# Twice the descriptor space for GpSimd's transfers, with a sum moved into a gate tile and a gate kept in PSUM

## The chip, the cores and the metric

The kernel runs on one core of a Trainium2 chip. The core has a matrix engine (TensorE), a vector engine (VectorE), a scalar engine (ScalarE), a general-purpose engine (GpSimd) and a synchronising engine (SyncE). They run side by side and wait for one another through semaphores. Data come from HBM by DMA; the transfers are started by SyncE, ScalarE or GpSimd and moved by 16 DMA engines. On the chip, data lie in SBUF (128 partitions) or in the 8 banks of PSUM, where TensorE puts its results. The metric is the device time of one execution in microseconds; less is better. The profile calls the engines PE (with PEld for its weight loads), DVE, ACT, POOL and SP.

## The reference

A trunk of two layers over 256 frames of 2048 channels. Layer 0 mixes the frames by gated linear attention, layer 1 by sparse attention over selected frames; behind each mixer stands a feed-forward block, and at the end a norm:

```python
for i in range(DEPTH):                      # DEPTH = 2
    h = rmsnorm(x, norm_mix[i])
    y = gla_mixer(h, ...) if i % 2 == 0 else dsa_mixer(h, ...)
    x = x + y
    x = x + swiglu(rmsnorm(x, norm_ffn[i]), ffn_w1[i], ffn_w3[i], ffn_w2[i])
return rmsnorm(x, norm_final)

def swiglu(h, w1, w3, w2):
    return (jax.nn.silu(h @ w1) * (h @ w3)) @ w2
```

w1 and w3 are 2048 x 5632, w2 is 5632 x 2048, all in float32. The change touches only the feed-forward block, `swiglu`.

## The kernel before

The program runs in order through gated attention (`gla`), feed-forward (`ffn`), sparse attention (`dsa`), feed-forward again, and the final norm; in the profile the two feed-forward stages lie at about 300 to 1080 us and 1460 to 2235 us. The program is written for a framework that places tiles, sets all semaphores and decides the order in which each engine gets its instructions. A pool gives out tiles by tag; tiles of one tag share its buffers, and a new one waits until the last reader of an older one is done.

Every product of float32 matrices is made of three matmuls on rounded halves. `split_w` (lines 133 to 141) makes the halves of a weight block of 512 x 512: ScalarE casts it to `wh` (line 137), VectorE subtracts to get `wl` (line 138). Both have three buffers; `raw` blocks that come from HBM have four (`RAW`).

The 5632 columns of w1 and w3 are cut into eleven blocks of 512. Two of them (1 and 5) are computed plainly by `plain_steps`. The other nine go through `pair` (lines 372 to 455), which computes h @ w1 and h @ w3 for both 128-row halves of the frames with seven products instead of eight, by sums and differences of the operands, in the manner of Strassen and Winograd. The forms of h that this needs (A11, A12, N7, F5, F6, F3, N22) are made once in `NormF.group`, where the tile f5 (line 327) is one of the helpers. The sums of weight blocks are made on the fly, half by half (c = 0, 1):

- `va` and `vb` are loaded (lines 423, 424); `plus` adds vb to va on VectorE (line 410).
- Product F5 uses va. As each half has been split, `plus_dma` (lines 417, 418) lets GpSimd start a DMA that adds another block of w3 to that half in place. Its result feeds product F6.
- `vc` and `vd` are streamed through `raw` (lines 435, 438). `minus` turns vb into another sum on VectorE (line 414).
- Product F6 uses va again, and again each half gets a block of w1 added by `plus_dma`, for product N22.

So each of the nine turns starts four accumulating transfers of 1 MB from GpSimd, two behind F5 and two behind F6. Over the two layers that is 36 pairs, 72 transfers.

The seven products collect in three PSUM banks, `b1`, `b2` and `b3`, out of four. The tile `y` (lines 432, 433) takes a copy of b2 after F5, and b3 is added to it after N7 (line 449). `gate` (lines 556 to 564) then makes silu(h @ w1) * (h @ w3): `done("11", b1)` and `done("12", w)` for the first 128 rows, `done("21", b3)` and `done("22", y)` for the second. It writes into tiles of tag "u" (two buffers, 2048 bytes a partition each). The gated tiles are transposed on TensorE (line 219, `split_t`) during the next turn and later multiplied with w2 in `pieces` (lines 515 to 538; matmuls 530 to 532). Between the products of a pair, `ffn` runs pieces or plain steps at slots listed in `turns`, so that TensorE has other work while sums are made.

Before the change, y has a buffer of its own of tag "y" in the pool of the stage (2048 bytes a partition), which f5 uses earlier. The program is built with `dynamic_dma_scratch_size=2048` (line 1158): the bytes a partition that are set aside for the descriptors of GpSimd's transfers.

Of the kernel before, what the change touches and what calls it, by code (L numbers as in the profile page):

```python
# [12 lines left out]
F32 = mybir.dt.float32  # L13
F32R = mybir.dt.float32r
BF16 = mybir.dt.bfloat16
AF = mybir.ActivationFunctionType
ALU = mybir.AluOpType
AX = mybir.AxisListType

P = 128  # L20
# [3 lines left out]
NB = 512  # L24
# [31 lines left out]
def trunk(  # L56
# [7 lines left out]
    nc = tc.nc  # L64
# [4 lines left out]
    cm = ctx.enter_context(tc.tile_pool(name="cm", bufs=2))  # L69
# [47 lines left out]
    def tick():  # L117

        while side:
            try:  # L120
                return next(side[0])
            except StopIteration:
                side.popleft()
# [9 lines left out]
    def split_w(raw, pool=wp):  # L133

        wh = pool.tile([P, 4, NB], F32R, tag="wh", bufs=3 if pool is wp else 1, name="wh")
        wl = pool.tile([P, 4, NB], F32R, tag="wl", bufs=3 if pool is wp else 1, name="wl")
        nc.scalar.copy(wh, raw)  # L137
        nc.vector.tensor_sub(wl, raw, wh.bitcast(F32))  # L138
        if sums_due:
            sums_due.popleft()()  # L140
        return wh, wl
# [83 lines left out]
    class Norm:  # L225
# [20 lines left out]
        def group(self, n):  # L246
            hi, lo = self.homes[n]
            for kk in range(2):
                tr = tr_p.tile([P, 2, SEQ], F32, tag="tr", name="tr")
                for t in range(NT):  # L250
                    for k in range(2):
                        c = (2 * kk + k) * P
                        nc.tensor.transpose(tr[:, k, t * P:(t + 1) * P], x[t][n][:, c:c + P], ident)
                gs = [cols[:, c:c + 1] for c in range(self.g0 + 4 * n + 2 * kk, self.g0 + 4 * n + 2 * kk + 2)]
                for k, g in enumerate(gs):
                    kt = 2 * kk + k
                    a = nc.scalar.activation(hi[:, kt, :], tr[:, k, :], AF.Copy, scale=g)
                for k, g in enumerate(gs):
                    kt = 2 * kk + k
                    v = nc.vector.scalar_tensor_tensor(lo[:, kt, :], tr[:, k, :], g, hi[:, kt, :].bitcast(F32),  # L260
                                                       op0=ALU.mult, op1=ALU.subtract)
                self.last = (a.ins, v.ins)
                if kk == 1:
                    self.parts[n] = (hi, lo, n * NB)
                yield
# [10 lines left out]
    class NormF(Norm):  # L276
# [21 lines left out]
        def group(self, n):  # L298
            j, c = divmod(n, 2)
            if c == 0:  # L300
                self.hx[j] = self.pool.tile([P, 2, 4, SEQ], F32, tag=("v0", "v1")[j], bufs=1, name="hx")
            for kk in range(2):
                tr = tr_p.tile([P, 2, SEQ], F32, tag="tr", name="tr")
                for t in range(NT):
                    for k in range(2):
                        f = (2 * kk + k) * P
                        nc.tensor.transpose(tr[:, k, t * P:(t + 1) * P], x[t][n][:, f:f + P], ident)
                for k in range(2):
                    col = self.g0 + 4 * n + 2 * kk + k
                    nc.scalar.activation(self.hx[j][:, c, 2 * kk + k, :], tr[:, k, :], AF.Copy,  # L310
                                         scale=cols[:, col:col + 1])
                yield
            a11, a21 = (self.hx[0][:, c, :, t * P:(t + 1) * P] for t in range(NT))

            def form(tag, l_, r_):
                f = self.pool.tile([P, 4, P], F32, tag=tag, bufs=1, name="form")
                nc.vector.tensor_sub(f, l_, r_)
                return f

            if j == 0:  # L320
                self.split("A11", c, a11)
                yield
                self.split("N7", c, form("s1", a11, a21))
                yield
                return
            a12, a22 = (self.hx[1][:, c, :, t * P:(t + 1) * P] for t in range(NT))
            f5 = form("y", a21, a22)
            self.split("F5", c, f5)
            f6 = form("w", a11, f5)
            self.split("A12", c, a12)  # L330
            yield
            self.split("F6", c, f6)
            f3 = form("s1", a12, f6)
            self.split("F3", c, f3)
            self.split("N22", c, a22, True)
            yield
# [35 lines left out]
    def pair(nrm, wa, wb, c0, turn, done):  # L372

        def src(w, j, c):
            r = j * 1024 + c * 512
            return w[r:r + 512, c0:c0 + NB].rearrange("(k p) n -> p k n", p=P)

        def load(w, j, homes):  # L380
            o = []
            for c, (pool, tag, bufs) in enumerate(homes):
                raw = pool.tile([P, 4, NB], F32, tag=tag, bufs=bufs, name=tag)
                nc.sync.dma_start(raw, src(w, j, c))
                o.append(raw)
            return o

        def product(acc, raws, form, start, stop, then=None):
            for c in range(2):
                wh, wl = split_w(raws[c])  # L390
                if then is not None:
                    then(c)
                hi, lo = nrm.forms[form]
                for j in range(4):
                    k = 4 * c + j
                    for i, (l_, r_) in enumerate(((hi, wh), (hi, wl), (lo, wh))):
                        nc.tensor.matmul(acc, l_[:, k, :], r_[:, j, :], start=start and k == i == 0,  # L397
                                         stop=stop and k == 7 and i == 2, skip_group_check=not start)
                    if j % 2:
                        tick()  # L400

        def bank():
            return acc_p.tile([P, NB], F32, tag="acc", name="acc")

        def sums(tag):
            return nrm.pool.tile([P, NB], F32, tag=tag, bufs=1, name=tag)

        def plus(dst, other):

            return lambda c: sums_due.append(lambda: nc.vector.tensor_add(dst[c], dst[c], other[c]))  # L410

        def minus(dst, other):

            return lambda c: sums_due.append(lambda: nc.vector.scalar_tensor_tensor(
                dst[c], dst[c], -1.0, other[c], op0=ALU.mult, op1=ALU.subtract))

        def plus_dma(dst, w, j):
            return lambda c: nc.gpsimd.dma_start(dst[c], src(w, j, c), accum_op=ALU.add)  # L418

        fz = nrm.pool  # L420
        stream = [(wp, "raw", RAW)] * 2
        homes = [((fz, "v0", 1), (fz, "v1", 1)), ((fz, "v2", 1), (res, "g3", 1))]
        va = load(wa, 0, homes[turn])
        vb = load(wb, 0, homes[1 - turn])
        b1 = bank()
        product(b1, va, "A11", True, True, plus(va, vb))
        b3 = bank()
        nc.scalar.mul(b3, b1, -1.0)
        yield
        b2 = bank()  # L430
        product(b2, va, "F5", True, True, plus_dma(va, wb, 1))
        y = sums("y")
        nc.scalar.copy(y, b2)
        yield
        vc = load(wb, 1, stream)
        product(b2, vc, "F3", False, True, minus(vb, vc))
        yield
        vd = load(wa, 1, stream)
        product(b1, vd, "A12", False, True)
        done("11", b1)  # L440
        yield
        product(b3, va, "F6", False, True, plus_dma(va, wa, 1))
        w = sums("w")
        nc.scalar.copy(w, b3)
        nc.vector.tensor_add(w, w, b2)
        done("12", w)
        yield
        product(b3, vb, "N7", False, True)
        nc.vector.tensor_add(y, y, b3)
        yield  # L450
        product(b3, va, "N22", False, True)
        done("21", b3)
        done("22", y)
        yield
        yield
# [84 lines left out]
    def ffn(layer, nrm):  # L540

        w1, w3, w2 = ffn_w1[layer], ffn_w3[layer], ffn_w2[layer]
        sc = {}
# [12 lines left out]
        def gate(us):  # L556
            def done(q, v):
                t = int(q[0]) - 1
                if q[1] == "1":
                    us[t] = cm.tile([P, NB], F32, tag="u", name="u")  # L560
                    nc.scalar.activation(us[t], v, AF.Silu, scale=sc["n" if t else "r"][:, t:t + 1])
                else:
                    nc.vector.scalar_tensor_tensor(us[t], us[t], sc["r"][:, t:t + 1], v, op0=ALU.mult, op1=ALU.mult)
            return done
# [28 lines left out]
        for turn, (b, at, items) in enumerate(turns):  # L593
            todo.extend(filler(i) for i in items)
            us = [None] * NT
# [573 lines left out]
```

## Time and profile before

| | us |
|---|---|
| median of 3 runs (2270.14 to 2272.52) | 2271.91 |
| the profiled execution | 2270.45 |
| its span, first to last instruction | 2268.6 |
| feed-forward of layer 0 (300 to 1080) | 780 |
| feed-forward of layer 1 (1460 to 2235) | 775 |

The profile gives for each engine the busy time. Idle time of an engine is put down to what ended it ("<-"). "DVE wl L138" is VectorE's instruction of line 138 that writes wl. A DMA's issue stands on the engine that issued it; the data land later. TensorE's matmuls overlap one another by a part of their length, so that a 512-column matmul is listed with about 0.39 us and follows the one before by 0.23. A row of a timeline has the start, the duration, engine, line, operation, what is written and read, the number of instructions merged into it, and in brackets the idle time before it and what ended it.

### The profile page before, as it was taken

The page shows a single profiled execution, that of the slowest core. Times are in us where ns is not written, and L with a number is a line of the kernel's source. Part 1 is how long each engine was busy: PE and PEld are TensorE (multiplying, and loading weights), DVE is VectorE, ACT ScalarE, POOL GpSimd, SP SyncE. Part 2 cuts the span into 40 slices and gives each one's busy share as a digit, 9 for nine tenths or more (in the row PEclk, how much of TensorE's full clock was granted, in tenths as well). Part 3 has the DMA queues.
Part 4 walks back from the last instruction along what each step waited for, and adds up shares of the span by engine and source line. Part 5 has one row for each costly group of instructions (what it writes and reads, how often), then busy time and mean ns, then how long its engine had stood idle before and what let it go on. Part 6 is the DMA issues. An engine that isn't in the chain of part 4 may idle for free. (4 is left out here: it accounts for less than half of the span.)

```text
span 2268.6 us, 25156 instructions
## 1 busy us (share of the span) xinstructions
PE 2218.0 (98%) x10151; PEld 1821.4 (80%) x10151; DVE 1585.1 (70%) x1200; ACT 1338.1 (59%) x1326; POOL 122.1 (5%) x165
## 2 busy tenths in 40 slices
PE   9999999999999999999999999999999999999997
PEld 7888888877888887777888888888787888787876
DVE  6546456887788778777655755558778787887785
ACT  5545355756666766666544544456576666666664
POOL 0000000100000000000100000000000000000000
PEclk9999999999999999999999999999999999999998
DMA  8555465887988798778554555557898889787973
GB/s 288 169 171 190 127 231 185 264 227 234 312 234 238 241 296 246 229 249 223 191 167 150 184 168 167 168 190 214 240 301 229 248 252 299 216 242 240 300 220 109
DMA packets 258998, 501.74 MB, mean 221 GB/s; under 512 B 8329, under 2 KB 20961, under 8 KB 258753
## 3 DMA queue, kind: packets, MB, share of 16 engines
q1 hardware_dynamic: 219856, 423.33, 53.4%
q0 software_dynamic: 38016, 75.50, 19.1%
q8 instruction: 79, 1.29, 0.2%
q10 hardware_dynamic: 1008, 1.31, 0.2%
q14 instruction: 39, 0.31, 0.0%
HBM read 497.98 MB, written 2.12 MB: 220 GB/s over the span
## 5 line engine op out<-in xcount | busy, mean ns | idle before, releaser
L138 DVE TENSOR_TENSOR wl<-raw,wh 128x2048 fp32r<-128x2048 f32 x185 | 421.1, 2289 | 165.3 <-ACT wh L137 164.0
L196 DVE TENSOR_TENSOR wl<-raw,wh 128x2048 fp32r<-128x2048 f32 (+3 forms) x147 | 317.6, 2164 | 276.0 <-ACT wh L195 275.9
L137 ACT CAST wh<-raw 128x2048 fp32r<-128x2048 f32 x185 | 353.4, 1913 | 140.3 <-PE half L474 39.2
L195 ACT CAST wh<-raw 128x2048 fp32r<-128x2048 f32 (+3 forms) x147 | 264.8, 1806 | 218.2 <-PE acc L207 197.7
L138 DVE TENSOR_TENSOR wl<-v,wh 128x2048 fp32r<-128x2048 f32 x132 | 300.6, 2287 | 63.5 <-ACT wh L137 63.1
L205 PE MATMUL acc<-wh,hh 128*128 128x512 f32 (+3 forms) x832 | 325.4, 391 | 0.0
L207 PE MATMUL acc<-wh,hl 128*128 128x512 f32 (+3 forms) x832 | 317.4, 381 | 0.0
L206 PE MATMUL acc<-wl,hh 128*128 128x512 f32 (+3 forms) x832 | 316.4, 380 | 0.6 <-DVE wl L196 0.6
L137 ACT CAST wh<-v 128x2048 fp32r<-128x2048 f32 x132 | 251.9, 1913 | 87.5 <-DVE v L410 24.9
L531 PE MATMUL down<-wl,g 128*128 128x512 f32 x640 | 250.6, 391 | 5.6 <-DVE wl L138 5.5
L530 PE MATMUL down<-wh,g 128*128 128x512 f32 x640 | 248.6, 392 | 2.6 <-ACT down L520 2.6
L532 PE MATMUL down<-wh,g 128*128 128x512 f32 x640 | 249.3, 389 | 0.0
L206 PEld LDWEIGHTS acc<-wl,hh 128*128 128x128 f32 x832 | 156.7, 188 | 29.6 <-issue 1.7
L207 PEld LDWEIGHTS acc<-wh,hl 128*128 128x128 f32 x832 | 156.3, 188 | 29.3
L205 PEld LDWEIGHTS acc<-wh,hh 128*128 128x128 f32 x832 | 156.5, 188 | 28.6 <-issue 1.9
L397 PE MATMUL acc<-wl,fhF 128*128 128x512 f32 x432 | 169.9, 393 | 7.3 <-DVE wl L138 7.3
L397 PE MATMUL acc<-wh,fhF 128*128 128x512 f32 x432 | 171.4, 397 | 4.2 <-ACT wh L137 2.4
L397 PE MATMUL acc<-wh,flF 128*128 128x512 f32 x432 | 168.4, 390 | 0.0
L138 DVE TENSOR_TENSOR wl<-g,wh 128x2048 fp32r<-128x2048 f32 x48 | 109.8, 2287 | 60.9 <-ACT wh L137 60.7
L531 PEld LDWEIGHTS down<-wl,g 128*128 128x128 f32 x640 | 120.1, 188 | 34.2 <-DVE wl L138 10.1
L530 PEld LDWEIGHTS down<-wh,g 128*128 128x128 f32 x640 | 120.1, 188 | 31.8 <-ACT down L520 7.0
L537 ACT COPY x<-down 128x512 f32<-128x512 f32 x112 | 65.4, 584 | 130.9 <-PE down L532 130.6
(283 smaller groups left out, 3776.7 us busy)
## 6 DMA issues: line engine op xcount, KB each, us to landing
raw<-in_ffn_w SPq DMA_DIRECT2D x192, 1024.0 KB, 7.7
v<-in_ffn_w SPq DMA_DIRECT2D x54, 1024.0 KB, 9.7
v<-in_ffn_w POOLq DMA_DIRECT2D x52, 1024.0 KB, 9.7
raw<-in_dsa_w_in SPq DMA_DIRECT2D x48, 1024.0 KB, 4.9
raw<-in_gla_w_in SPq DMA_DIRECT2D x40, 1024.0 KB, 5.1
g<-in_ffn_w POOLq DMA_DIRECT2D x20, 1024.0 KB, 13.2
g<-in_ffn_w SPq DMA_DIRECT2D x18, 1024.0 KB, 6.5
raw<-in_gla_w_out SPq DMA_DIRECT2D x16, 1024.0 KB, 5.0
```

The source lines that it names most:

```text
L137: nc.scalar.copy(wh, raw)
L138: nc.vector.tensor_sub(wl, raw, wh.bitcast(F32))
L195: a = nc.scalar.copy(wh[:, sl, :n], raw[:, sl, :n])
L196: v = nc.vector.tensor_sub(wl[:, sl, :n], raw[:, sl, :n], wh[:, sl, :n].bitcast(F32))
L205: nc.tensor.matmul(acc[t][:, :n], hi[:, k, ts_], wh[:, k, :n], start=start, stop=False)
L206: nc.tensor.matmul(acc[t][:, :n], hi[:, k, ts_], wl[:, k, :n], start=False, stop=False)
L207: nc.tensor.matmul(acc[t][:, :n], lo[:, k, ts_], wh[:, k, :n], start=False, stop=last)
L397: nc.tensor.matmul(acc, l_[:, k, :], r_[:, j, :], start=start and k == i == 0, stop=stop and k == 7 and i == 2, skip_group_check=not start)
L530: nc.tensor.matmul(acc[t], hi[:, k, ts_], wh[:, k, :], start=False, stop=False, skip_group_check=True)
L531: nc.tensor.matmul(acc[t], hi[:, k, ts_], wl[:, k, :], start=False, stop=False, skip_group_check=True)
L532: nc.tensor.matmul(acc[t], lo[:, k, ts_], wh[:, k, :], start=False, stop=last, skip_group_check=True)
L537: nc.scalar.copy(x[t][n], acc[t])
```

## The change

The space for descriptors goes from 2048 to 4096 bytes a partition. The tag "y" of the stage's pool goes: f5 and y take a tile of tag "u" from the pool `cm`, which has two buffers. The gate of the second 128 rows no longer takes a tile of "u": silu is applied in the PSUM bank b3 itself, and the product is written over y, which is then what gets transposed. The instructions are the same in kind and number.

```diff
-            def form(tag, l_, r_):
-                f = self.pool.tile([P, 4, P], F32, tag=tag, bufs=1, name="form")
+            def form(tag, l_, r_, pool=None):
+                f = (pool or self.pool).tile([P, 4, P], F32, tag=tag, bufs=2 if pool else 1, name="form")
                 nc.vector.tensor_sub(f, l_, r_)
                 return f
...
-            f5 = form("y", a21, a22)
+            f5 = form("u", a21, a22, cm)
...
         product(b2, va, "F5", True, True, plus_dma(va, wb, 1))
-        y = sums("y")
+        y = cm.tile([P, NB], F32, tag="u", name="u")
         nc.scalar.copy(y, b2)
...
             def done(q, v):
                 t = int(q[0]) - 1
-                if q[1] == "1":
+                if q == "21":
+                    nc.scalar.activation(v, v, AF.Silu, scale=sc["n"][:, 1:2])
+                    us[t] = v
+                elif q == "22":
+                    nc.vector.scalar_tensor_tensor(v, v, sc["r"][:, 1:2], us[t], op0=ALU.mult, op1=ALU.mult)
+                    us[t] = v
+                elif q[1] == "1":
                     us[t] = cm.tile([P, NB], F32, tag="u", name="u")
                     nc.scalar.activation(us[t], v, AF.Silu, scale=sc["n" if t else "r"][:, t:t + 1])
                 else:
                     nc.vector.scalar_tensor_tensor(us[t], us[t], sc["r"][:, t:t + 1], v, op0=ALU.mult, op1=ALU.mult)
...
-    nc = bacc.Bacc("TRN2", target_bir_lowering=False, num_devices=1, dynamic_dma_scratch_size=2048)
+    nc = bacc.Bacc("TRN2", target_bir_lowering=False, num_devices=1, dynamic_dma_scratch_size=4096)
```

## The prediction

> **What bounds the kernel now.** I read the page first, then the engine windows of the two feed-forward stages, TensorE's waits, and the timeline around single waits.
>
> ```profile
> span 2268.6 us, 25156 instructions
> PE 2218.0 (98%) x10151; PEld 1821.4 (80%) x10151; DVE 1585.1 (70%) x1200; ACT 1338.1 (59%) x1326; POOL 122.1 (5%) x165
> ...
> q0 software_dynamic: 38016, 75.50, 19.1%
> ```
>
> TensorE bounds the whole. Only its 50.6 us of idle time (2268.6 - 2218.0) can be won, since the change takes no matmul away. The change touches the two stages that run `ffn`:
>
> ```profile
> 300.00:1080.00 780.00, 763.48 (x3397) 623.60 (x3396) 593.36 (x341) 498.30 (x437) 48.92 (x42) 1.00 0.82 244
> 1460.00:2235.00 775.00, 756.88 (x3351) 616.53 (x3349) 587.43 (x339) 497.52 (x444) 48.08 (x38) 1.00 0.82 241
> ```
>
> Behind the stretch and its length stand the busy times of TensorE, its weight loads, VectorE, ScalarE and GpSimd, the granted clock, the DMA share and GB/s. TensorE idles 16.5 + 18.1 = 34.6 us there, at a granted clock of 1.00. Its waits name the causes:
>
> ```profile
> PE acc L397 <- DVE wl L138: 10.9, 12, 1.8
> PE acc L397 <- ACT wh L137: 6.3, 8, 2.6
> PE tr L219 <- DVE u L563: 5.5, 2, 2.8
> PE down L531 <- DVE wl L138: 5.5, 6, 1.2
> ...
> PE down L530 <- ACT down L520: 2.6, 3, 1.5
> ```
>
> wh and wl are the two halves of a weight block, made by ScalarE (L137) and VectorE (L138). To see why they are late I follow one wait back, from GpSimd's accumulating transfers (L418) to TensorE.
>
> ```profile
> 2172.07 2.28 DVE L138 TENSOR_TENSOR wl<-g,wh 128x2048 fp32r<-128x2048 f32 x1
> ...
> 2172.56 1.31 POOL L418 DMA_DIRECT2D v<-in_ffn_w  x1 [36.55 <-DVE wl L138]
> 2181.48 1.29 POOL L418 DMA_DIRECT2D g<-in_ffn_w  x1 [7.61 <-DMA v<-in_ffn_w]
> ...
> DMA to landing us min/median/max: 8.6/11.0/13.3
> ...
> 2194.88 1.91 ACT L137 CAST wh<-g 128x2048 fp32r<-128x2048 f32 x1 [2.98 <-DMA g<-in_ffn_w]
> ...
> 2196.82 2.29 DVE L138 TENSOR_TENSOR wl<-g,wh 128x2048 fp32r<-128x2048 f32 x1 [2.48 <-ACT wh L137]
> ...
> 2199.17 0.50 PE L397 MATMUL acc<-wl,fhF 128*128 128x512 f32 x1 [0.71 <-DVE wl L138]
> ```
>
> Each product issues two such transfers of 1 MB, one for each half. The second could go when wl of g is done, at 2172.07 + 2.28 = 2174.35. It goes at 2181.48, 0.3 us after the first landed (2172.56 + 8.6), though it writes another tile. It lands at 2181.48 + 13.3 = 2194.8; ScalarE has stood for it 2.98 us, cast and subtraction follow, and TensorE waits 0.71 us. All 36 pairs look so: no second transfer starts before the first has landed. GpSimd has room for one at a time. That is the resource the change doubles.
>
> **The sum of waits that hang on it.** Of the 23 waits of L397 and L530 (10.9 + 6.3 + 2.6 = 19.8 us) twelve stand directly behind the landing of a second transfer: at 466.0 and 468.3, the last at 2199.17, 16.0 us together. The other eleven, 3.8 us, are each under 0.7 us, and no landing precedes them.
>
> ```profile
> 465.96 0.51 PE L397 MATMUL acc<-wh,fhN 128*128 128x512 f32 x1 [2.64 <-ACT wh L137]
> 468.29 0.68 PE L397 MATMUL acc<-wl,fhN 128*128 128x512 f32 x1 [1.82 <-DVE wl L138]
> ```
>
> **Doubling the space.** By the trace one transfer fits in 2048 bytes, so two fit in 4096. In the example the second is issued some 6.5 us earlier: 2174.35 + about 0.6 (2172.56 was 0.4 behind its own subtraction; the first's 1.3 us of issue lie ahead of it). How much earlier it lands depends on the DMA engines:
>
> ```profile
> 2174.60:2181.20 6.60, 6.38 (x31) 4.99 (x30) 6.60 (x5) 5.22 (x5) 0.00 (x0) 1.00 1.05 172
> 2181.20:2185.70 4.50, 4.50 (x22) 3.72 (x20) 3.16 (x2) 1.58 (x3) 1.29 (x1) 1.00 0.99 331
> 2185.70:2194.80 9.10, 9.10 (x41) 7.37 (x40) 6.70 (x3) 6.13 (x5) 0.00 (x0) 1.00 1.08 274
> ```
>
> The engines are full throughout: first the accumulating transfer almost alone (172), then SyncE's loads alone (331), then both (274). Issued early, the second follows the first at 2181.2 and shares from there. Bounds: 0 earlier, if the loads stay first, to 6.5, the hold itself. If it gets the share of the third stretch, it needs the same 9.1 us and lands 4.5 us earlier, the length of the loads' own stretch; if the loads' backlog takes half of that back, 2.3. I take 3.5, between them. Then the twelve waits end so: the pair at 466/468 (4.46) loses 3.5; all others are at most 3.1 together at one landing and go. Recovered: 16.0 - 1.0 = **15.0 us**.
>
> The Trainium skill says, in "DMA: Bandwidth & Descriptors", section "Issuing engines are not separate DMA queues", that transfers of all issuing engines run on the same 16 DMA engines and that starting them from several engines saves only the time of initiating. By that rule a full DMA would give the loads' time back in full, and the sum would be near 0; the 1.05, 0.99 and 1.08 agree that it is full here.
>
> **What the loads lose.** The price is theirs. In the third stretch 274 x 9.1 = 2.49 MB moved, 1.05 of them the transfer's, 1.44 the loads'. A load of 1 MB beside it therefore takes 9.1 x 1.05 / 1.44 = 6.6 us of that stretch.
>
> ```profile
> 2179.42 0.37 SPq L384 DMA_DIRECT2D raw<-in_ffn_w  x1
> ...
> DMA to landing us min/median/max: 5.0/5.0/5.0
> ...
> 2185.71 3.72 ACT L137 CAST wh<-raw 128x2048 fp32r<-128x2048 f32 x2
> ...
> 2187.65 4.50 DVE L138 TENSOR_TENSOR wl<-raw,wh 128x2048 fp32r<-128x2048 f32 x2 [3.29 <-ACT wh L137]
> ...
> 2192.86 0.39 PE L397 MATMUL acc<-wl,fhA 128*128 128x512 f32 x1
> ```
>
> This load lands at 2184.4 now, and at 2181.2 + 6.6 = 2187.8 then. Its cast, the second of the two, starts at 2185.71 + 3.72 - 1.91 = 2187.5 anyway; its wl ends at 2192.15 and is needed at 2192.86. So it bears 3.1 + 0.7 = 3.8 us, and loses 3.4: no wait, with 0.4 to spare. Ten loads of `vd` lie so, the first at 421.83; at 0 to 0.5 us each, I charge 0.3, **3 us** in all.
>
> **Waits that stay.** The six of L531 (5.5 us) come from a third load:
>
> ```profile
> 814.84 1.91 ACT L137 CAST wh<-raw 128x2048 fp32r<-128x2048 f32 x1 [5.96 <-DMA raw<-in_ffn_w]
> ...
> 804.42 6.82 DVE L138 TENSOR_TENSOR wl<-raw,wh 128x2048 fp32r<-128x2048 f32 x3 [0.73 <-ACT wh L137]
> ...
> 815.15 0.39 PE L397 MATMUL acc<-wl,fhA 128*128 128x512 f32 x1
> ...
> 804.30:814.00 9.70, 9.70 (x44) 8.05 (x43) 6.79 (x3) 4.33 (x4) 0.00 (x0) 1.00 1.06 269
> ```
>
> By 814.84 both accumulations and three loads must be through full engines (1.06), in whatever order. I count 0 for these; 5.5 is the upper end. The two waits of L219 (5.5) are the end of a stage and stay.
>
> **The moved tiles.** No instruction is added or taken away.
>
> ```profile
> L563 DVE SCALAR_TENSOR_TENSOR u<-u,rstd,y 128x512 f32<-128x512 f32 x18 | 13.4, 746 | 1.3 <-ACT u L561 1.3
> ...
> L489 DVE SCALAR_TENSOR_TENSOR early<-early,rstd,half 128x512 f32<-128x512 f32 x4 | 3.0, 741 | 0.0
> ...
> L433 ACT COPY y<-acc 128x512 f32<-128x512 f32 x18 | 10.6, 588 | 14.1 <-PE acc L397 14.1
> L428 ACT ACTIVATE acc<-acc 128x512 f32<-128x512 f32 x18 | 10.5, 581 | 5.9 <-PE acc L397 5.6
> ```
>
> The gate of the second half (L563) will read PSUM: L489 does so in 741 ns against 746. Silu will write PSUM: L428 writes it in 581 ns, L433 SBUF in 588. 0 us. Two lifetimes grow. y takes a buffer of "u" until the transposes (L219) have read it, so the next `copy` (L433) waits for them; behind it on ScalarE stand the casts. The bank of b3 is held until L563, and the next F5 product may need it.
>
> ```profile
> 2175.20 0.60 PE L219 MATMUL tr<-ident,u 128*128 128x128 f32 x4
> ...
> 2178.59 0.59 ACT L433 COPY y<-acc 128x512 f32<-128x512 f32 x1 [0.80 <-PE acc L397]
> ...
> 2084.11 0.75 DVE L563 SCALAR_TENSOR_TENSOR u<-u,rstd,y 128x512 f32<-128x512 f32 x1
> ...
> 2089.13 0.50 PE L397 MATMUL acc<-wh,fhF 128*128 128x512 f32 x1 [0.35 <-ACT wh L137]
> ```
>
> These are the narrowest places: 2.8 us from transposes to copy, 4.3 us from gate to product. Both are covered: 0 us. The f5 tile gets a second buffer and nothing waits for it.
>
> **Sum.** 15.0 - 3 = 12 us off the profiled execution's 2270.45 us (span 2268.6 and 1.85 around it): 2258.5. The median of the runs, 2271.91, is 1.46 above that execution, so 2271.91 - 12 = **2260 us**.
>
> **Rivals.** *Full engines, only the order changes.* The loads give back what the transfers win: the loads' delay passes 3.8 us by about 1.5 at the ten places (15 us), and nothing is left. For it: DMA shares of 0.99 to 1.08. Against: the twelve waits are few and the loads have slack. 2272.
>
> *Slower: the second transfer keeps the loads out.* If it goes wholly ahead, it needs 1.05 MB at 172, 6.1 us behind 2181.2, and the load 2.7 more (1.05 MB at 388 GB/s, where loads run alone): it lands at 2190.0 instead of 2184.4, 5.6 late. That is 1.8 us over the 3.8, at ten places 18. At the six places of L531 the second load has no more than the 3.9 us between its wl, the third of the row at 804.42 (ended 811.24), and the matmul at 815.15: 1.7 over, 10 more. 28 - 15 = 13 us slower: 2285. It decides from a delay of 3.8 us. Against: loads and transfer shared the third stretch, 1.44 MB to 1.05.
>
> ```profile
> 800.40:804.30 3.90, 3.90 (x19) 3.21 (x18) 3.29 (x2) 3.42 (x5) 1.30 (x1) 1.00 1.03 388
> ```
>
> *The space is not what holds it.* Then nothing changes: 2272. For it: the hold might be a semaphore. Against: the second transfer writes another tile than the first. A transfer leaves 38016 / 72 = 528 packets, 33 on each DMA engine. The Trainium skill ("DMA: Bandwidth & Descriptors", "The descriptor swizzle") has 9 read and 9 write descriptors per engine for 1 MiB, of 16 bytes ("Terms"); an estimate from it puts seven such transfers in 2048 bytes, and by that this rival would hold. The 33 packets contradict its count here.
>
> *All goes.* The twelve waits and L531's: 16.0 + 5.5 = 21.5 less: 2250.
>
> **Chances.** Forecast (2254 to 2267) 0.65, all goes 0.08, full engines 0.11, space not the hold 0.05, slower 0.11. 0.2% is 4.5 us, about what a measurement of this kernel can tell from no change. Faster 0.73, same 0.16, slower 0.11. The range goes from 2250 to 2272: it takes in the cases of no change, and leaves out the slower one.
>
> **What would show it.** Right: second transfers issued 2 to 4 us behind the first, before it lands; in the accumulating pairs ScalarE's casts of v and g no longer wait for DMA; L397 <- wh, wl and L530 <- L520 fall from 19.8 to some 5 us; L531 stays near 5.5. Loads of `vd` landing over 3.8 us later speak for the slower rival. Unchanged gaps of 8 to 9 us between the two issues mean that the space was not the hold. A copy of y that waits for L219, or an F5 product that waits for L563, would show the moved tiles wrong. The order of each engine's instructions is fixed when the program is built; if the new buffers change it, other waits of a few us may come or go, and the sum is off by them.

## The result, and the profile after

The changed kernel takes 2260.06 us (median of 4 runs, 2258.83 to 2260.71) against 2272.22 for the kernel before beside it: a ratio of 0.9946, 95% interval 0.9929 to 0.9963, or 8 to 16 us. The two profiled executions differ by 9.7 us (2270.45 and 2260.71, spans 2268.6 and 2258.9). Each engine gets the same instructions in the same order in both programs, but for a transpose in each feed-forward stage, three small loads of the attention stage and a block of the last product, which stand a few places earlier or later; the gate of the second 128 rows writes and reads other tiles, as the change has it. So the difference is one of waiting.

The profile page of the kernel after: its span, busy times and the queue of GpSimd's transfers:

```profile
span 2258.9 us, 25154 instructions
...
PE 2216.3 (98%) x10151; PEld 1821.7 (81%) x10151; DVE 1585.6 (70%) x1200; ACT 1340.9 (59%) x1326; POOL 121.7 (5%) x165
...
q0 software_dynamic: 38016, 75.50, 19.2%
```

TensorE idles 42.6 us instead of 50.6. The same two stretches in the engine windows (TensorE's busy time is the second number):

```profile
300.00:1080.00 780.00, 766.13 (x3411) 626.02 (x3410) 596.15 (x343) 500.21 (x438) 48.69 (x42) 1.00 0.82 246
1460.00:2235.00 775.00, 761.95 (x3365) 621.44 (x3365) 589.97 (x342) 496.76 (x438) 47.87 (x38) 0.99 0.81 242
```

More matmuls fit into each stretch (3411 and 3365, before 3397 and 3351). TensorE's waits after (total, times, longest):

```profile
PE acc L397 <- DVE wl L138: 14.6, 20, 1.5
PE tr L219 <- DVE u L563: 5.8, 3, 2.7
...
PE acc L397 <- ACT wh L137: 2.3, 6, 0.6
PE acc L397 <- ACT u L433: 1.8, 8, 0.2
PE down L531 <- DVE wl L138: 1.4, 2, 0.7
```

L530's waits are gone, L531's fell from 5.5 to 1.4, L397's for wh from 6.3 to 2.3. But L397's for wl **rose**, from 10.9 to 14.6. The four groups were 25.3 us and are 18.3. The groups of L397 by form show that these are not the same waits. Behind the bar stand the idle time ahead of the group and what ended it; fhF is read by F3, F5 and F6, fhA by A11 and A12, fhN by N7 and N22. The kernel before:

```profile
L397 PE MATMUL acc<-wl,fhF 128*128 128x512 f32 x432 | 169.9, 393 | 7.3 <-DVE wl L138 7.3
...
L397 PE MATMUL acc<-wl,fhA 128*128 128x512 f32 x288 | 113.7, 395 | 0.0
L397 PE MATMUL acc<-wl,fhN 128*128 128x512 f32 x288 | 113.7, 395 | 3.6 <-DVE wl L138 3.6
...
L397 PE MATMUL acc<-wh,fhN 128*128 128x512 f32 x288 | 113.4, 394 | 3.9 <-ACT wh L137 3.9
```

The kernel after:

```profile
L397 PE MATMUL acc<-wl,fhF 128*128 128x512 f32 x432 | 168.9, 391 | 1.3 <-DVE wl L138 1.3
...
L397 PE MATMUL acc<-wl,fhA 128*128 128x512 f32 x288 | 116.3, 404 | 13.3 <-DVE wl L138 13.3
...
L397 PE MATMUL acc<-wh,fhN 128*128 128x512 f32 x288 | 112.0, 389 | 0.0
L397 PE MATMUL acc<-wl,fhN 128*128 128x512 f32 x288 | 112.0, 389 | 0.0
```

F6 and N22, which use what the transfers bring, no longer wait; what is left at fhF are small waits that both kernels have. A12, which uses the loads of `vd`, and A11 never waited and now wait 13.3 us: A12 10.6 at thirteen places, A11 1.3 at each of two (473.34 and 1621.92). Some of what such waits cost stands as busy time, too: the group of 288 has 116.3 us instead of 113.7.

A wait can also cost something behind itself. In the kernel before, this is the stretch right behind N22's waits of 2.64 and 1.82 us, the second of which ends at 468.29:

```profile
468.50:471.90 3.40, 3.40 (x9) 2.66 (x9) 3.37 (x2) 1.49 (x1) 0.00 (x0) 0.51 0.72 224
```

The granted clock is 0.51 there, and in the timeline the matmuls follow one another by 0.43 us instead of 0.23. By an estimate from this row it costs 3.4 x 0.5 = 1.7 us. In the kernel after, the clock of this stretch is 1.00. In the second layer both kernels have such a stretch: before 0.50 from 1622.2, behind N22's waits; after 0.51 from 1622.7, behind A11's wait of 1.33 us. The mean of 1.00 over a whole stage does not show them.

The turn of the prediction's example, in the timeline of the kernel after:

```profile
2163.88 1.28 POOL L418 DMA_DIRECT2D v<-in_ffn_w  x1 [42.84 <-DVE wl L138]
2166.07 1.28 POOL L418 DMA_DIRECT2D g<-in_ffn_w  x1 [0.92 <-DVE wl L138]
...
2170.74 0.37 SPq L384 DMA_DIRECT2D raw<-in_ffn_w  x1
...
2180.45 1.91 ACT L137 CAST wh<-raw 128x2048 fp32r<-128x2048 f32 x1 [1.47 <-DMA raw<-in_ffn_w]
...
2182.39 2.29 DVE L138 TENSOR_TENSOR wl<-raw,wh 128x2048 fp32r<-128x2048 f32 x1 [1.09 <-ACT wh L137]
...
2184.74 0.50 PE L397 MATMUL acc<-wl,fhA 128*128 128x512 f32 x1 [0.39 <-DVE wl L138]
```

The second transfer goes 2.2 us behind the first (before: 8.9). The trace has its landing at 2179.23, 15.4 us behind the first's issue (before: 22.2). Over the 18 pairs behind F5 the median fell from 22.5 to 16.4 us, behind F6 from 23.0 to 16.3. The load of `vd`, issued 6.9 us behind the first transfer in both kernels, lands 16.5 us behind it (2180.35) instead of 11.9 (2184.4): 4.6 later, 0.8 beyond the 3.8 it could bear, and TensorE waits 0.39.

The DMA queues of the kernel after from 2174.9 to 2178.2, packets, MB and share of time of each queue, show how the two share (q0 carries GpSimd's transfers, q1 SyncE's loads):

```profile
DMA packets 427, 0.87 MB, mean 263 GB/s; under 512 B 3, under 2 KB 3, under 8 KB 427
...
q0 software_dynamic: 210, 0.42, 69.1%
q1 hardware_dynamic: 217, 0.44, 40.1%
```

The two move packet for packet, 210 to 217, but an accumulating packet takes 69.1 / 210 against 40.1 / 217 of the time, 1.8 times as long. Beside a transfer the loads get 0.44 MB in 3.3 us, 133 GB/s, a third of what loads get alone (388). The Trainium skill says in "DMA: Bandwidth & Descriptors", section "Queues, rings and completion order", that each DMA engine takes the queues that have work in turn, a packet from each; the 210 and 217 agree.

### The profile page after: what moved, and what is told of

The parts are those of the page before. It is cut to its first block, busy times and chain, and to the rows that moved or that the text cites. A ratio compares the mean times of both kernels' runs of the same rounds, so it can differ in the third digit from the quotient of the medians.

```text
span 2258.9 us, 25154 instructions
## 1 busy us (share of the span) xinstructions
PE 2216.3 (98%) x10151; PEld 1821.7 (81%) x10151; DVE 1585.6 (70%) x1200; ACT 1340.9 (59%) x1326; POOL 121.7 (5%) x165
## 4 chain that ended last, share of the span: by engine, by line
PE 71%; DVE 12%; DMA 8%; issue 5%; ACT 4%; SPq 0%; POOL 0%; ACTq 0%; DVEq 0%; POOLq 0%
PE acc L397 17%; PE acc L205 11%; PE acc L207 11%; PE acc L206 11%; DMA raw<-in_ffn_w 7%; DVE wl L138 7%; PE half L474 5%; PE down L530 4%; PE down L531 4%; PE down L532 4%; ACT wh L137 3%; DVE v L410 2%; DVE v L414 1%; PE trq L906 0%; PE po L765 0%
## 5 line engine op out<-in xcount | busy, mean ns | idle before, releaser
L531 PE MATMUL down<-wl,g 128*128 128x512 f32 x640 | 249.6, 390 | 1.4 <-DVE wl L138 1.4
L530 PE MATMUL down<-wh,g 128*128 128x512 f32 x640 | 248.0, 391 | 0.0
L397 PE MATMUL acc<-wh,fhF 128*128 128x512 f32 x432 | 171.4, 397 | 4.1 <-ACT wh L137 2.3
L397 PE MATMUL acc<-wl,fhF 128*128 128x512 f32 x432 | 168.9, 391 | 1.3 <-DVE wl L138 1.3
L397 PE MATMUL acc<-wh,flF 128*128 128x512 f32 x432 | 168.3, 390 | 0.0
L530 PEld LDWEIGHTS down<-wh,g 128*128 128x128 f32 x640 | 120.2, 188 | 27.7 <-ACT down L520 2.9
L531 PEld LDWEIGHTS down<-wl,g 128*128 128x128 f32 x640 | 120.1, 188 | 26.9 <-DVE wl L138 2.6
L532 PEld LDWEIGHTS down<-wh,g 128*128 128x128 f32 x640 | 120.1, 188 | 24.7
```

Source lines behind the costliest of these rows:

```text
L530: nc.tensor.matmul(acc[t], hi[:, k, ts_], wh[:, k, :], start=False, stop=False, skip_group_check=True)
L531: nc.tensor.matmul(acc[t], hi[:, k, ts_], wl[:, k, :], start=False, stop=False, skip_group_check=True)
L532: nc.tensor.matmul(acc[t], lo[:, k, ts_], wh[:, k, :], start=False, stop=last, skip_group_check=True)
```

## The experiments

**What carries the gain: space or moved tiles?** Three kernels, each compared with the kernel before on the same chip; dots stand for what is left out of a line or between lines.

```diff
 tiles_only: the kernel after
-... dynamic_dma_scratch_size=4096)
+... dynamic_dma_scratch_size=2048)
 space_2112: the kernel before
-... dynamic_dma_scratch_size=2048)
+... dynamic_dma_scratch_size=2112)
 space_3072: the kernel after
-... dynamic_dma_scratch_size=4096)
+... dynamic_dma_scratch_size=3072)
```

> The kernel after with 2048 instead of 4096 bytes for descriptors; the moved tiles stay. Theory (the space alone carries the gain): the second transfer of each pair is issued about 0.3 us behind the landing of the first again, the waits of TensorE behind L138 and L137 in L397 come back to about 17 us, and the time is that of the kernel before, 2272 us, within 2. Rival (the moved tiles carry it, since y and f5 have two buffers now): the time stays at 2260, whatever the second transfers do.

> The kernel before, nothing moved, with 2112 instead of 2048 bytes for descriptors. A transfer leaves 33 packets on each DMA engine. If what one transfer takes is between 1024 and 1056 bytes, two fit here and the time is that of the kernel after, 2260 us, with second issues 2 to 4 us behind the first. If one takes more than 1056 bytes, the second is held as before and the time stays at 2272. The Trainium skill (DMA: Bandwidth & Descriptors, Terms) has 16 bytes for a descriptor; an estimate from it and from 33 packets, each with a read and a write descriptor, is 33 x 2 x 16 = 1056 bytes for one transfer, 2112 for two, by which this size would just do.

> The kernel after with 3072 bytes. If one transfer takes at most 1536 bytes, the second goes as early as in the kernel after (2 to 4 us behind the first) and the time is 2260 us. If it takes more, the second is held until the first has given part of its space back: issued somewhere between 4 and 8.9 us behind the first, and the time lies between 2260 and 2272.

Measured: tiles_only 2271.5 us, ratio 0.9999 (0.9990 to 1.0008). space_2112 2261.59, 0.9956 (0.9943 to 0.9969). space_3072 2260.01, 0.9948 (0.9936 to 0.9959). The moved tiles alone give nothing; 64 bytes a partition more in an otherwise untouched kernel give what the whole change gives, within the intervals. GpSimd's queue in the timelines shows it directly, first tiles_only:

```profile
2176.50 1.31 POOL L418 DMA_DIRECT2D v<-in_ffn_w  x1 [37.23 <-DVE wl L138]
2185.80 1.29 POOL L418 DMA_DIRECT2D g<-in_ffn_w  x1 [8.00 <-DMA v<-in_ffn_w]
```

and space_2112:

```profile
2166.31 1.28 POOL L418 DMA_DIRECT2D v<-in_ffn_w  x1 [42.85 <-DVE wl L138]
2168.51 1.30 POOL L418 DMA_DIRECT2D g<-in_ffn_w  x1 [0.92 <-DVE wl L138]
```

They are 9.3 us apart in the one, 2.2 in the other. If both transfers of a pair take the same, one of 33 packets per DMA engine thus takes more than 1024 and at most 1056 bytes; two missed the 2048 by at most 64. By the Trainium skill's 16 bytes for a descriptor ("DMA: Bandwidth & Descriptors", "Terms") an estimate is 33 x 2 x 16 = 1056, and the measured bounds agree with it.

In five turns of the kernel before, and of tiles_only, the space also held F6's first transfer: it went 0.3 us behind the landing of F5's second (at 2195.09 before, at 2199.87 in tiles_only).

One of the five runs of space_2112 took 12,730 us, so it was run again, beside a size with room to spare (only the number in the line differs).

> The kernel before with 2112 bytes once more, since one of its five runs took 12,730 us. If the size that just fits two transfers has a fault of its own, such a run comes again; if it was an accident of that run, all five lie within 3 us of 2261.

> The kernel before, nothing moved, with 2304 bytes: room for two transfers and 192 bytes to spare, if one takes between 1024 and 1056. The same as with 2112 and 4096: 2260 to 2262 us, and no run far off.

Measured: space_2112_again 2262.28 us (2259.91 to 2263.53, six runs), 0.9962 (0.9947 to 0.9977); space_2304 2260.95 (2259.18 to 2262.69), 0.9958 (0.9945 to 0.9972). The long run did not come again; what it was stays open.

**Holding the second transfers by program.** GpSimd reads one column of the first half between the two transfers, with the space of the kernel after:

```diff
-        def plus_dma(dst, w, j):
-            return lambda c: nc.gpsimd.dma_start(dst[c], src(w, j, c), accum_op=ALU.add)
+        def plus_dma(dst, w, j, hold):
+            return lambda c: (c and hold and nc.gpsimd.tensor_copy(seen, dst[0][:, 0, 0:1]), nc.gpsimd.dma_start(dst[c], src(w, j, c), accum_op=ALU.add))
```

> The kernel after, 4096 bytes, but GpSimd reads one column of the first half behind the first transfer, so that the second is issued only when the first has landed, in F5 and in F6. Theory (what counts is that the second starts before the first has landed): the gain goes, 2272 us, within 2, and TensorE's waits are those of the kernel before. Rival (the larger space does something else too, in the way descriptors are made or moved): 2260 to 2266.

Measured: 2280.33 us, 1.0037 (1.0025 to 1.0049), outside of what theory and rival had. GpSimd's queue in its timeline shows that nothing is held:

```profile
421.08 1.51 POOL L418 DMA_DIRECT2D v<-in_ffn_w  x1 [15.06 <-DVE wl L138]
423.26 1.29 POOL L418 DMA_DIRECT2D g<-in_ffn_w  x1 [0.67 <-DVE wl L138]
429.88 2.08 POOL L418 COPY seen<-v 128x1 f32<-128x1 f32 x1 [5.33 <-DMA v<-in_ffn_w]
```

The framework put the read behind the second transfer: in all 36 pairs the second goes 1.6 to 3.7 us behind the first, much as in the kernel after. Yet the kernel is 20 us slower than that one. What it had besides was a new tile of 4 bytes a partition (`seen`), which pad_4 adds alone:

```diff
+    ... sm.tile([P, 1], F32, tag="seen", bufs=1, name="seen")
```

> The kernel after with one unused tile of 4 bytes a partition more, placed where hold_both had the tile for its column; no instruction is added. Theory (hold_both, with TensorE busy 2244 us against 2216, was slowed by the addresses of the tiles behind, shifted by 4 bytes): the time is 2272 to 2282, with TensorE busy some 2240. Rival (GpSimd's 36 reads slowed it): 2260 and 2216.

Measured: 2278.69 us, 1.0037 (1.0023 to 1.0051), with no instruction more than the kernel after and the same order on every engine. The groups of TensorE by form in pad_4, in stages that the change doesn't touch:

```profile
L205 PE MATMUL acc<-wh,hh 128*128 128x512 f32 x736 | 298.6, 406 | 0.0
L207 PE MATMUL acc<-wh,hl 128*128 128x512 f32 x736 | 291.8, 396 | 0.0
L206 PE MATMUL acc<-wl,hh 128*128 128x512 f32 x736 | 291.4, 396 | 0.2 <-DVE wl L196 0.2
```

The kernel after has 401, 391 and 390 ns in these rows (295.0, 288.1 and 287.2 us). With the unused tile these matmuls are 5 to 6 ns longer; all in all TensorE is busy 2244.2 us instead of 2216.3, and idle 32.4 instead of 42.6. What is left for a cause is the place of the tiles behind it, which the 4 bytes shift; that is argued, since no run moved one tile alone. The following kernels write the column to a tile that exists already, and order the second transfer behind the read. No run holds the second transfers of both products in this way, so that the larger space does nothing else is not tested by itself.

**F5's transfers and F6's, one at a time.**

> The kernel after, but behind F5 GpSimd reads one column of the first half (2.08 us by the run hold_both) between the two transfers, and the second stands behind that read: it is issued some 2.1 us behind the landing of the first, 1.8 later than in the kernel before. F6's pair stays early. Theory (F5's early second transfers are what makes the loads of vd late): of the 14.6 us of waits behind loads the 12.0 behind vd fall to the 5.5 of the kernel before or less, and the five waits behind F5's second landings, 5.9 us before, come back 0 to 1.8 longer each: 2260 - 6.5 + 5.9 to 14.9, so 2259 to 2268 us. Rival (F6's transfers make the loads late): the 12.0 stay and the 5.9 come on top, 2266 to 2275.

> The same read between the two transfers of F6 alone; F5's pair stays early. Theory: the waits behind F6's second landings come back (four of L397, 7.6 us, three of L530, 2.6 us in the kernel before; up to 1.8 longer each), the two waits behind loads of the next turn's first blocks (1.3 us each in the kernel after, at 473 and 1622) go, and the 12.0 behind vd stay: 2260 + 10.2 - 2.6, up to 7 more, so 2268 to 2275 us. Rival (F6's part gave nothing): 2260.

Measured: hold_f5 2260.13 us, 0.9957 (0.9943 to 0.9971): the same as the kernel after. hold_f6 2287.25, 1.0072 (1.0059 to 1.0084). TensorE by form in hold_f5 (L394 is L397 here):

```profile
L394 PE MATMUL acc<-wh,fhF 128*128 128x512 f32 x432 | 173.1, 401 | 10.0 <-ACT wh L137 8.2 <-ACT u L433 1.8
L394 PE MATMUL acc<-wl,fhF 128*128 128x512 f32 x432 | 172.0, 398 | 10.0 <-DVE wl L138 10.0
...
L394 PE MATMUL acc<-wl,fhA 128*128 128x512 f32 x288 | 113.7, 395 | 0.1
```

and in hold_f6:

```profile
L394 PE MATMUL acc<-wl,fhA 128*128 128x512 f32 x288 | 115.4, 401 | 11.4 <-DVE wl L138 11.4
L394 PE MATMUL acc<-wl,fhN 128*128 128x512 f32 x288 | 114.5, 398 | 12.0 <-DVE wl L138 12.0
...
L394 PE MATMUL acc<-wh,fhN 128*128 128x512 f32 x288 | 113.2, 393 | 5.2 <-ACT wh L137 5.2
```

With F5's second held, the waits of A12 and A11 are gone (13.3 to 0.1) and F6's come in their place (wl 1.3 to 10.0, wh 2.3 to 8.2): the sum stays. So A12 waits because of F5's early transfer. This hold is later than that of the kernel before, though: 5.0 and 4.5 us of F6's waits lie in the first turn of each layer, where the second goes 12.9 and 12.8 us behind the first (before: 9.3 and 9.8). In the kernel before, F6's waits behind second landings were 5.9 us, so against it F5's early transfers cost more (13.3) than they bring there, even if the 4.1 us less at L531 are theirs. With F6's second held, A12's waits stay. N22's come back, larger than before the change (17.2 against 7.5), and L530 and L531 wait 6.3 us. F6's early transfer is what the change gains by. The 2287.25 lies 12 beyond the 2268 to 2275 that I gave: I had counted only the places that waited before, and new ones came: N22 in three more turns of each layer, 1.0 to 1.6 us each, where the read puts the second transfer 1.6 to 2.0 us later than in the kernel before.

**A place between.** F5's second transfer behind the copy of y:

```diff
-        product(b2, va, "F5", True, True, plus_dma(va, wb, 1))
+        add = plus_dma(va, wb, 1)
+        product(b2, va, "F5", True, True, lambda c: add(c) if c == 0 else None)
         y = cm.tile([P, NB], F32, tag="u", name="u")
         nc.scalar.copy(y, b2)
+        seen = nc.gpsimd.tensor_copy(warm[:, 0:1], y[:, 0:1])
+        with behind((seen.ins,)):
+            add(1)
```

> The kernel after, but F5's second transfer goes behind the copy of y (L433) by way of a read of one column of y on GpSimd: issued some 6.5 us later than in the kernel after, some 9 earlier than in the kernel before. Theory (the give-back is the price of starting the transfer while the loads of vd are on the way, and the transfer has room to spare): the loads land some 3 us earlier, most of the 12.0 us of waits behind them go, the transfer still lands before or little behind its cast, 2251 to 2257 us. Rival (no room: what the loads win, the transfer loses): 2259 to 2266.

Measured: 2259.24 us, 0.9947 (0.9934 to 0.9961): on average the rival. The place is not quite where the expectation had it: the second transfers go 6.4 to 12.9 us behind the first, by the median as late as in the kernel before (9.6 against 9.4), since the read of y took from 0.18 to 6.94 us. In ten of the 18 turns they go as late as in hold_f5 (within 0.4 us), in eight 2.2 to 4.9 earlier. Among these eight are the four later turns in which F6 waits 1.15 to 1.50 us in hold_f5; here it doesn't.

The waits lie in two turns of each layer only. In the first turns F6 waits 4.4 us (444 to 447) and 4.7 (1593 to 1595): the read of y took 5.24 us there, and the transfer of the first layer came at 428.4 instead of 418. (Six reads of 6.9 us in other turns have no such wait behind them.) In the second turns TensorE waits 2.0 us (509 to 511) and 2.3 (1659 to 1660), behind casts that stood 4.3 and 4.5 us for a load. The other seven have no wait over 0.4 us. The first turns are better off early (A12 waits 1.2 and 1.1 us in the kernel after, and A11 behind it 1.3 each), the second ones held (no wait in hold_f5). So mixed gives each of the three kinds of turn its own place (`add` as in late_f5):

```diff
+        product(b2, va, "F5", True, True, add if c0 == 0 else lambda c: add(c) if c == 0 else None)
...
+        if c0:
+            seen = nc.gpsimd.tensor_copy(warm[:, 0:1], va[0][:, 0, 0:1] if c0 == 2 * NB else y[:, 0:1])
+            with behind((seen.ins,)):
+                add(1)
```

> The kernel after, with F5's second transfer by turn: early in the first turn of each layer (as in the kernel after), behind the landing of the first in the second turn (as in hold_f5), behind the copy of y in the other seven (as in late_f5). F6's stay early. Theory (each of the three runs shows, turn by turn, what its place costs, and the turns hardly touch one another): late_f5's 18.9 us of waits lose the 9.2 of the first turns and the 4.3 of the second ones, and the first turns bring 2.3 to 4.9 behind their loads: 7.7 to 10.3 us against 18.3 to 20 in the kernel after, so 2250 to 2253 us. Rival (a wait that goes in one turn comes back in the next): 2257 to 2261.

Measured: **2246.52 us**, 0.9888 (0.9868 to 0.9908), faster than both kernels and a little better than expected. TensorE's waits in mixed:

```profile
PE acc L394 <- DVE wl L138: 7.1, 10, 1.5
...
PE acc L394 <- ACT wh L137: 2.3, 6, 0.6
PE acc L394 <- ACT u L429: 1.8, 8, 0.2
```

These are 11.2 us, against 20.1 in the kernel after (14.6, 2.3, 1.4 and the 1.8 behind L433). The time fell by more, 13.5. About half of the rest is in the busy time of one group: wl with fhA has 114.2 us against 116.3.

The expectation went by late_f5's waits alone and left out what lay behind them, here in late_f5:

```profile
446.60:450.00 3.40, 3.40 (x8) 2.72 (x9) 3.40 (x2) 1.73 (x1) 1.30 (x1) 0.50 1.14 236
511.40:514.80 3.40, 3.40 (x9) 2.62 (x8) 3.40 (x2) 0.31 (x1) 1.28 (x1) 0.50 0.92 287
1593.40:1600.20 6.80, 5.18 (x12) 4.12 (x13) 6.05 (x3) 3.50 (x3) 1.29 (x1) 0.50 1.11 232
```

These stretches stand at the waits of the first and second turns. TensorE was busy 12.0 us in them at a granted clock of 0.50, which by an estimate from these rows loses 6 us. In mixed these waits are gone, and the clock is 1.00 from 440 to 470, 500 to 530, 1580 to 1610 and 1625 to 1680. That this is why mixed came out better than expected is argued.

The same order without the moved tiles, in the kernel before with 2304 bytes:

> The order of mixed (F5's second transfer early in the first turn of each layer, behind the landing of the first in the second, behind the copy of y in the others) in the kernel before with 2304 bytes: y keeps its own tile and the second half's gate its own tile of u. Theory (the moved tiles are worth nothing here either): 2245 to 2249 us, as mixed. Rival (mixed needs the buffers of u or the gate in PSUM): over 2252.

Measured: 2245.67 us, 0.9892 (0.9876 to 0.9909). The tiles need not move for this either.

## Why the prediction was right, and where its terms were not

- **What holds the second transfer** is the space: right, shown by tiles_only and space_2112. The rival "space is not the hold" is out. The Trainium skill's count ("DMA: Bandwidth & Descriptors", "The descriptor swizzle": 9 read and 9 write descriptors) did not fit these transfers; 33 of each do.
- **Issue 2 to 4 us behind the first**: right, a median of 2.2 us behind F5 and 2.7 behind F6.
- **Second landings 3.5 us earlier** (bounds 0 to 6.5): 6.2 behind F5 and 6.8 behind F6, at the upper bound and just over it. I let transfer and loads share as in the third stretch, 1.05 MB to 1.44. In fact the second transfer follows the first without a gap, and the loads beside it get packet for packet (0.42 MB to 0.44).
- **15.0 us recovered from twelve waits**: all twelve went, 16.0 us. The 1.0 I left at 466 went too. The sum had no term for the clock: by the stages' mean of 1.00 I took it as full, and the 1.7 us of half clock behind the waits at 466 and 468 were not in it.
- **3 us lost by the loads**: the term that was mis-sized. Loads of `vd` land 4.6 us later in the example, not 3.4, and 5.5 to 6.5 in the turns where they are issued 3.8 us behind the transfer (11.5 to 17.7 in one of them). The margin of 3.8 is passed, and A12 waits 10.6 us; A11, which had no term, waits 2.6. The mechanism is that of the rival "slower", with its point of decision. Its price was smaller than I had it (13.3 us, not 28): 18 was too much for A12, and its second part, 10 us more behind a third load, did not come.
- **L531 stays at 5.5 us**: wrong, 1.4. Its third load lands 22.7 us behind the first transfer where it landed at 23.6 (the turn at 790 to 815), and TensorE comes later to it by its wait for `vd`. That these two make up the difference is argued; no run isolates it. hold_f5 shows only that it goes as well when that load lands at 18.5.
- **The moved tiles at 0 us**: right, shown by tiles_only, and by 2260.95 with 2304 bytes in the kernel before.
- **The sum.** By the waits it is 16.0 + 4.1 - 13.3 = 6.8 us, not 12. The profiled execution gained 9.7: 1.2 more are other waits (idle 8.0 in all), 1.7 busy time. The medians gained 12.2, with an interval of 8 to 16. The mechanism and the direction were right; the size was met partly by luck, since errors of both signs fell together.
- **The rival of the full engines**, by which the loads give back what the transfers win, holds for half of the change: F5's early transfer takes from the loads at least what it gives. F6's has a gain. That no urgent load lies beside F6's is argued: A11's waits (2.6 us) go in hold_f5 and in hold_f6 alike. The Trainium skill's rule ("DMA: Bandwidth & Descriptors", "Issuing engines are not separate DMA queues") is that the transfers of all issuing engines run on the same 16 DMA engines; the loads that land 4.6 us later agree.

## What to carry to other kernels

Where a GpSimd transfer is issued only when the one before has landed, and no data tie them, look at the space for descriptors: it goes by whole transfers, and here at most 64 bytes too few held every second transfer. Starting a transfer earlier takes from whatever shares the DMA engines with it, so give each transfer its own place by who waits next, and measure turn by turn: here one rule for all turns gave 2259 to 2260 us, three rules 2246. Look at the granted clock right behind long waits, in windows of a few us, before you price a wait by its length alone. When an experiment adds a tile, even an unused one, check first that the instructions far from the change still have their durations.

## What was not expected of the hardware

One tile of 4 bytes a partition, without any instruction, cost 18.6 us (2260.06 to 2278.69), with matmuls of 512 columns 5 to 6 ns longer each in rows that have nothing to do with it. The Trainium skill ("SBUF — State Buffer", "Operand start alignment") has addresses at multiples of 4 bytes as legal for float32 and says that its runs timed nothing. Which operand's address matters was not tried.

A read of one column on GpSimd took from 0.18 to 6.94 us in late_f5. The trace shows where the long ones end, here one of them and VectorE beside it:

```profile
569.70 6.92 POOL L431 COPY warm<-u 128x1 f32<-128x1 f32 x1 [4.40 <-ACT u L430]
...
569.89 4.48 DVE L138 TENSOR_TENSOR wl<-raw,wh 128x2048 fp32r<-128x2048 f32 x2
574.30 2.28 DVE L410 SCALAR_TENSOR_TENSOR v<-v,raw 128x2048 f32<-128x2048 f32 x1
```

The read ends at 576.62, VectorE's run of instructions at 576.58. All thirteen reads of over 0.3 us in late_f5 end so, 0.04 to 0.05 us behind the end of a VectorE instruction, and VectorE is busy for 99% or more of each. The other five took 0.18 us while VectorE was busy as well; why they got through is not shown.
